# A block's last 16 keys: transposes and value matmuls over all 128 rows

## The chip, the cores and the metric

The kernel runs on one core of one Trainium2 chip. The metric is the time of one execution on the device in microseconds (us). The median of three runs of the kernel before is 1477.79 us (1477.2 to 1480.66). Engines are named as in the profile: PE (TensorE, matmuls), PEld (its weight loads), DVE (VectorE), ACT (ScalarE), POOL (GpSimd), SP (SyncE, which issues most DMAs).

## The reference

Two layers over 1040 tokens (16 learned ones and 1024 of the input) of width 1024. Each layer has a gated linear attention (GLA) and a sparse attention side by side; the part that matters here is the sparse attention:

```python
TOPK_MAX = 256; Q_BLOCK = 128; DSA_HEADS = 8; DSA_KV_HEADS = 2; DSA_HD = 64; N_META = 16
# for each block of 128 queries
score = einsum('bqj,bqjs->bqs', iw * 8 ** -0.5, relu(dots))          # indexer, all causal keys
_, sel = lax.top_k(score, topk)                                      # 256 keys of each query
s = einsum('bqgrd,bqkgd->bqgrk', qg, k_sel) * (DSA_HD ** -0.5)
p = softmax(where(valid, s, -inf))
o = einsum('bqgrk,bqkgd->bqgrd', p, v_sel)
# then: out projection, x <- LayerNorm(alpha * x + y)
```

The kernel does not gather: it computes all causal scores and gives the keys that were not selected a bias that makes their weight zero.

## The kernel before

The queries after the 16 learned tokens lie in 8 blocks `i` of 128. Block `i` sees 144 + 128 i keys: i + 1 whole blocks of 128 keys and a tail of 16, since keys are counted from token 0 and queries from token 16. The heads go in 4 pairs `hp`, so that a layer has 32 units `(i, hp)`, and the program 64. A unit has two stages:

- `stage_a` (line 1002): scores by matmuls (L1033, tile `S`), bias and row extreme on DVE (L1034), exponent on ACT (L1040). It leaves the weights of two heads in `Pt[0]`, `Pt[1]`: 128 rows (queries) by 144 + 128 i columns (keys).
- `stage_b` (line 1045), two units later: for every two key blocks, transposes of 128x128 pieces on PE (L1058, tile `PT`), a rounded copy `ph` on ACT (L1061), the remainder `pl` on DVE (L1062), and value matmuls of 128 contraction rows and 256 columns for each (L1064, L1065, tile `o`). Values `va[k]` stand with the rounded half in columns 0 to 63 and the remainder in 64 to 127.

The tail of 16 keys comes last in `stage_b` (lines 1066 to 1076). Only the last 32 queries of a block can see it, for the tail's first key is token 128 (i+1) and query row `r` is token 16 + 128 i + r. So the kernel takes rows 96 to 127 alone: two transposes of 32 rows and 16 columns (L1068, tile `PTe`, written 16x32), ACT copy and DVE remainder of 16x64 into one buffer `pe` (L1070, L1071), and two value matmuls of 16 contraction rows and 64 moving columns (L1074) that close the accumulation of `pos`. `pe` comes from the pool `v`, of which there are three buffers (`NV = 3`); the copies `ot` (L1077) and `rx` (L1086) come from it too.

Between the units PE has other work of the same layer to fill in: the gate projections `wz` (L356 to L358) and the first half of the output projection, `yg` and `yp` (L1128 to L1130). Products in single precision are made of three matmuls each, over a rounded part and a remainder.

The order of the instructions on each engine is not that of the code: a scheduler simulates the program while it is built and lets each engine's queue be filled in the order in which instructions become ready there. PE runs its queue in that order. Values are loaded by `vat` (lines 886 to 899): the last 16 keys' values are written to rows 0 to 15 of their piece alone (`m = 16`).

`rtok` (line 174) is a table of 144 columns in the tile of constants `cst` that the indexer's keys are rotated with, on DVE, at the start of each layer (L478 to L483). `r_g` is a large region that many stages use in turn: columns 3072 to 4095 hold the last of nine row tiles in the layer norms.

Of the kernel before, what the change touches and what calls it, by code (L numbers as in the profile page):

```python
# [10 lines left out]
F32 = mybir.dt.float32  # L11
F32R = mybir.dt.float32r
# [5 lines left out]
AF = mybir.ActivationFunctionType  # L18
OP = mybir.AluOpType
# [5 lines left out]
L = 1040  # L25
# [51 lines left out]
METAX = 21  # L77
METAL = 4
SWAP = 0
CST = 2450  # L80
NSEC = 5
FPRI = 4000
SELN = 256
# [15 lines left out]
def trunk(ctx: ExitStack, tc, a, out, dbg=None, stop=None):  # L99
    nc = tc.nc  # L100
    V, S, G, T, Q = nc.vector, nc.scalar, nc.gpsimd, nc.tensor, nc.sync
    dbg = dbg or {}

    const = ctx.enter_context(tc.tile_pool(name="const", bufs=1))
# [30 lines left out]
    def vu(name, dt=F32):  # L135
        return unit("v", dt)
# [6 lines left out]
    r_g = const.tile([128, 9328], F32, name="r_g")  # L143
# [14 lines left out]
    def small(n, dt=F32, parts=1):  # L158
        o = cofs[0]
        cofs[0] = o + n  # L160
        assert cofs[0] <= CST
        return cst[:, o:o + n].bitcast(dt) if dt != F32 else cst[:, o:o + n]

    ident = small(128)
# [6 lines left out]
    lmi = u("lmi", I32)[:, :448].rearrange("p (a b) -> p a b", a=7)  # L171
    Q.dma_start(lmi, a["lmask"])
    V.tensor_copy(lmask, lmi)
    rtok = small(144).rearrange("p (i j f) -> p i j f", i=2, j=9)
    Q.dma_start(rtok, a["rtok"])
    ropec, ropes = small(260), small(260)
    Q.dma_start(ropec, a["ropec"])
    Q.dma_start(ropes, a["ropes"])
# [33 lines left out]
    Q.dma_start(seltab, a["seltab"])  # L212
    selz, selc, selcap, selact = [seltab[:, 7 * x:7 * x + 7] for x in range(4)]
    iota8 = seltab[:, 28:36]
    nlev = [0]
    rr = [0, 0, 0, 0, 0, 0]
    sofs = [0]
    for i in range(NB):
        sofs.append(sofs[i] + (144 + 128 * i if i else 0))

    X = const.tile([128, 2, 8, L], F32R, name="X")
    h_dram = dpool.tile([L, D], F32, name="h_dram")
    z_dram = dpool.tile([8, 128, L], F32, name="z_dram")
    r_dram = dpool.tile([L, D], F32, name="r_dram")
# [187 lines left out]
    for l in range(DEPTH):  # L412
# [15 lines left out]
        for c0, n in GB:  # L428
            for f in range(2):
                p = sc("glog")  # L430
                T.matmul(p[:, :n], wg2[64:80, 128 * f:128 * f + 128], misc[64:80, c0:c0 + n], start=True, stop=True)
                e = log_sigmoid_parts(p[:, :n], bg[:, f:f + 1], 128, n)
                m = u("gmin")
# [14 lines left out]
        for j0, j1 in ((0, 5), (5, 9)):  # L448
            p = tr("mT")
# [6 lines left out]
            pv = p[:, 88 * (ja - j0):88 * (j1 - j0)].rearrange("p (j f) -> p j f", f=88)  # L456
            V.tensor_copy(ktm[:, ja:j1, :], pv[:, :, 0:64])
            V.tensor_scalar(iwt[:, ja:j1, :], pv[:, :, 80:88], 8 ** -0.5, 0.125, OP.mult, OP.mult)
        ikg = ikg_s
        for i, nm in enumerate(("idx_g", "idx_b")):  # L460
            v = a[nm][l]
            Q.dma_start(ikg[:, i, :], bass.AP(tensor=v.tensor, offset=v.offset, ap=[[0, 128], [1, 64]]))
# [25 lines left out]
        for js in ((0, 1, 2, 3, 4), (5, 6, 7, 8)):  # L488
            p = tr("ikT")
# [378 lines left out]
        with tc.high_priority(offset=SELPRI):  # L868
# [3 lines left out]
            for i in blks:  # L872
                W, x = 144 + 128 * i, slice(i - 1, i)
# [13 lines left out]
        va = []  # L887
        for k0, k1 in ((0, 4), (4, 5), (5, 8), (8, 9)):
            p = tr("vT")
            nk = k1 - k0  # L890
            m = 128 if k0 < 8 else 16
            o = 256 * (k0 % 5)
            vt = vat[k0 // 5][:, o:o + 256 * nk].rearrange("p (k g d) -> p k g d", g=2, d=128)
            va += [vt[:, k] for k in range(nk)]
            for k in range(k0, k1):
                T.transpose(p[:m, 128 * (k - k0):128 * (k - k0) + 128], avr[:, 128 * k:128 * k + m], ident)
            pv = p[:m, :128 * nk].rearrange("p (k g d) -> p k g d", k=nk, g=2)
            S.activation(vt[:m, :, :, 0:64], pv, AF.Copy)
            V.tensor_tensor(vt[:m, :, :, 64:128], pv, vt[:m, :, :, 0:64].bitcast(F32), OP.subtract)
# [145 lines left out]
        def stage_b(i, hp):  # L1045

            W, t0, g = 144 + 128 * i, NM + 128 * i, hp // 2
            b = ctxs[i]
            mx, oc, zt, Pt = b["mx"], b["oc"], b["zt"], b[hp]
            nk = i + 1  # L1050
            po = bank("o", NO, "o")
            pos = po[:, :256]
            for k0 in range(0, nk, 2):
                kk = min(2, nk - k0)
                p = pt_("PT")
                for x in range(kk):
                    for hh in range(2):
                        T.transpose(p[:, 256 * x + 128 * hh:256 * x + 128 * hh + 128],  # L1058
                                    Pt[hh][:, 128 * (k0 + x):128 * (k0 + x) + 128], ident)
                ph, pl = u("ph", F32R), u("pl", F32R)  # L1060
                S.activation(ph[:, :256 * kk], p[:, :256 * kk], AF.Copy)  # L1061
                V.tensor_tensor(pl[:, :256 * kk], p[:, :256 * kk], ph[:, :256 * kk].bitcast(F32), OP.subtract)  # L1062
                for x in range(kk):
                    T.matmul(pos, va[k0 + x][:, g, :], ph[:, 256 * x:256 * x + 256], start=(k0 + x == 0), stop=False)  # L1064
                    T.matmul(pos, va[k0 + x][:, g, :], pl[:, 256 * x:256 * x + 256], start=False, stop=False)  # L1065
            p = pt_("PTe")
            for hh in range(2):
                T.transpose(p[:16, 32 * hh:32 * hh + 32], Pt[hh][96:128, W - 16:W], ident[96:128, 96:128])  # L1068
            pe = vu("pe", F32R)
            S.activation(pe[:16, 0:64], p[:16, :64], AF.Copy)  # L1070
            V.tensor_tensor(pe[:16, 64:128], p[:16, :64], pe[:16, 0:64].bitcast(F32), OP.subtract)  # L1071
            pov = pos.rearrange("p (h t) -> p h t", h=2)
            for s in range(2):
                T.matmul(pov[:, :, 96:128], va[nk][:16, g, :],  # L1074
                         pe[:16, 64 * s:64 * s + 64].rearrange("p (h t) -> p h t", h=2),
                         start=False, stop=(s == 1))
            tt = vu("ot")  # L1077
            S.activation(tt[0:64, :256], po[64:128, :256], AF.Copy)
            for odd in range(2):
                V.tensor_tensor(oc[64 * odd:64 * odd + 64, hp, :], po[0:64, 128 * odd:128 * odd + 128],  # L1080
                                tt[0:64, 128 * odd:128 * odd + 128], OP.add)
            if hp < 3:
                return
            V.reciprocal(mx[:, :, 5:6], mx[:, :, 4:5])
            pr = pt_("rb")
            rx = vu("rx")  # L1086
            G.tensor_scalar(rx.rearrange("p (h d) -> p h d", h=8), mx[:, :, 5:6].to_broadcast([128, 8, 64]),
                            1.0, 0.0, OP.mult, OP.add)
            for j in range(4):
                T.transpose(pr[:, 128 * j:128 * j + 128], rx[:, 128 * j:128 * j + 128], ident)  # L1090
            prv = pr.rearrange("p (h t) -> p h t", h=4)
            if i < NDEF:
                V.tensor_tensor(oc, prv, oc, OP.mult)
                Q.dma_start(o_dram[i].rearrange("p (h t) -> p h t", h=4), oc)
                return
            V.tensor_tensor(zt, prv, zt, OP.mult)
            G.tensor_tensor(oc, oc, zt, OP.mult)
            S.activation(X[:, 0, 4:8, t0:t0 + 128], oc, AF.Copy)  # L1098
            G.tensor_tensor(X[:, 1, 4:8, t0:t0 + 128], oc, X[:, 0, 4:8, t0:t0 + 128].bitcast(F32), OP.subtract)
# [32 lines left out]
        for qd in range(NQ):  # L1132
            w = wunits(a["w_out"][l, qd], 256, 2, "wo", (0, 1))
            for j in tiles:
# [4 lines left out]
                p = bank("yg", NYG, "yg")[:n, :256]  # L1139
# [16 lines left out]
        for qd in range(2):  # L1156
            w = wunits(a["w_out"][l, qd], 256, 2, "wo", (2, 3))
            for j in tiles:
                t0, n = tok(j)
                p = pj("yp")[:n, :256]  # L1160
# [8 lines left out]
        for j in tiles:  # L1169
            t0, n = tok(j)  # L1170
            p = pj("yp")[:n]
# [99 lines left out]
```

## Time and profile before

| | us |
|---|---|
| median of three runs | 1477.79 |
| the profiled execution | 1479.79 |
| its span, first to last instruction | 1478.0 |
| PE busy | 1377.4 (93%) |
| weight loads busy | 1283.4 (87%) |
| DVE busy | 1040.1 (70%) |
| ACT busy | 791.7 (54%) |
| POOL busy | 721.3 (49%) |
| granted TensorE clock, mean | 0.974 |

The profiled execution is 2.0 us above the median; 1.8 us of it lie outside the span. The two attention stages, in which the units run, go from about 430 to 712 us and from about 1155 to 1421 us. A PE record's duration includes time in which the next matmul already runs, so the busy share of PE is no measure of how much it does; the distance from one start to the next is.

### The profile page before, as it was taken

To read this page: it belongs to the slowest core of one execution; us is meant where nothing else is said; L and a number is where in the kernel's file an instruction comes from. 1 tells how busy PE (TensorE), PEld (TensorE's weight loads), DVE (VectorE), ACT (ScalarE), POOL (GpSimd) and SP (SyncE) were. 2 spreads that over 40 slices of the span, in tenths; PEclk is the share of its full clock that TensorE was granted. 3 is DMA by queue.
4 is the path that set the end of the run, shared out by engine and by line. 5 is a ranking of instruction groups with operands and counts; after the bars stand their busy time and mean duration, and the time that the engine had idled before them with its cause. 6 is when DMAs were issued, how large, how long until landed. Compare 5 with 4: busy or idle time off the path is not lost. (4 is left out here: it accounts for less than half of the span.)

```text
span 1478.0 us, 27238 instructions
## 1 busy us (share of the span) xinstructions
PE 1377.4 (93%) x9471; PEld 1283.4 (87%) x9471; DVE 1040.1 (70%) x2440; ACT 791.7 (54%) x1815; POOL 721.3 (49%) x662
## 2 busy tenths in 40 slices
PE   2988998899999999999999889988999999999985
PEld 2878998788899988898999889987899999899985
DVE  8569997866534566776597699978665455778638
ACT  5446623544377777653254564254445877776412
POOL 6534422988643457222363441349785344652134
PEclk9999999999999999999999999999999999999998
DMA  7243322333243455215233432231433343621522
GB/s 256 105 133 87 93 96 77 98 95 117 83 126 116 120 149 141 67 48 165 70 128 109 133 99 74 94 104 51 146 101 105 103 135 108 186 90 51 158 69 114
DMA packets 143166, 162.63 MB, mean 110 GB/s; under 512 B 19552, under 2 KB 112496, under 8 KB 143024
## 3 DMA queue, kind: packets, MB, share of 16 engines
q1 hardware_dynamic: 112656, 125.73, 28.9%
q10 hardware_dynamic: 30368, 35.12, 6.9%
q8 instruction: 75, 1.23, 0.3%
q14 instruction: 67, 0.55, 0.1%
HBM read 104.76 MB, written 56.04 MB: 109 GB/s over the span
## 5 line engine op out<-in xcount | busy, mean ns | idle before, releaser
L323 POOL TENSOR_TENSOR w<-w 128x512 fp32r<-128x512 f32 (+1 forms) x134 | 181.3, 1354 | 294.2 <-ACT w L322 232.5
L322 ACT ACTIVATE w<-w 128x512 fp32r<-128x512 f32 (+1 forms) x134 | 83.5, 625 | 112.7 <-DMA w<-in_w_fm_dram 48.2
L543 DVE SCALAR_TENSOR_TENSOR r_sc<-v,cst,r_sc 128x346 f32<-128x346 f32 (+6 forms) x196 | 124.5, 689 | 5.8 <-ACT v L538 4.8
L356 PE MATMUL wz<-X,w 128*128 128x346 f32 (+1 forms) x384 | 125.9, 328 | 0.3
L357 PE MATMUL wz<-X,w 128*128 128x346 f32 (+1 forms) x384 | 125.0, 326 | 0.0
L358 PE MATMUL wz<-X,w 128*128 128x346 f32 (+1 forms) x384 | 124.6, 324 | 0.0
L1062 DVE TENSOR_TENSOR u<-PT,u 128x512 fp32r<-128x512 f32 (+1 forms) x160 | 100.7, 633 | 31.4 <-ACT u L1061 21.5
L1061 ACT ACTIVATE u<-PT 128x512 fp32r<-128x512 f32 (+1 forms) x160 | 86.0, 545 | 61.5 <-PE PT L1058 57.3
L635 POOL TENSOR_TENSOR qb<-r_g,u 64x256 f32<-64x256 f32 (+1 forms) x144 | 114.9, 798 | 5.6
L1040 ACT ACTIVATE r_g<-r_g,cst 128x272 f32<-128x272 f32 (+7 forms) x128 | 99.7, 780 | 10.7 <-DVE cst L1034 10.2
L538 ACT ACTIVATE v<-dots 128x346 f32<-128x346 f32 (+5 forms) x224 | 86.4, 461 | 16.3 <-PE dots L536 10.6
L1058 PE MATMUL PT<-cst,r_g 128*128 128x128 f32 x576 | 88.8, 277 | 0.0
L646 DVE COPY_PREDICATED r_g<-cst,lev 128x512 f32<-128x512 uint8 (+1 forms) x72 | 52.9, 735 | 50.1 <-PE lev L642 49.3
L570 PE MATMUL gvp<-w,X 128*128 128x256 f32 (+1 forms) x288 | 81.8, 289 | 1.5 <-ACT w L322 1.5
L629 POOL TENSOR_TENSOR r_g<-r_g,u 128x256 f32<-128x256 f32 (+1 forms) x60 | 49.6, 826 | 67.9 <-PE lev L642 40.5
L572 PE MATMUL gvp<-w,X 128*128 128x256 f32 (+1 forms) x288 | 82.6, 288 | 0.0
L571 PE MATMUL gvp<-w,X 128*128 128x256 f32 (+1 forms) x288 | 82.3, 287 | 0.0
L1033 PE MATMUL S<-ak,aq 128*128 128x346 f32 (+7 forms) x240 | 80.1, 340 | 0.2
L642 PE MATMUL lev<-qb,r_g 128*128 128x128 f32 (+1 forms) x480 | 66.8, 277 | 11.2 <-POOL qb L635 11.2
L642 PEld LDWEIGHTS lev<-qb,r_g 128*128 128x128 f32 (+1 forms) x480 | 60.0, 189 | 17.9 <-POOL qb L635 12.7
L1034 DVE CUSTOM_DVE_ANT_0 r_g<-S,r_kb 128x456 f32<-128x456 f32 (+6 forms) x112 | 55.9, 519 | 27.1 <-PE S L1033 20.2
L1128 PE MATMUL yp<-w,X 128*128 128x256 f32 (+1 forms) x238 | 69.1, 292 | 5.6 <-ACT X L1098 5.6
(351 smaller groups left out, 4966.0 us busy)
## 6 DMA issues: line engine op xcount, KB each, us to landing
w<-in_w_fm_dram SPq DMA_DIRECT2D x88, 256.0 KB
r_g<-aq_dram SPq DMA_DIRECT2D x64, 128.0 KB
w<-in_w_out_dram SPq DMA_DIRECT2D x32, 256.0 KB
r_sc<-h_dram SPq DMA_DIRECT2D x53, 128.0 KB
h_dram<-r_g SPq DMA_DIRECT2D x12, 512.0 KB
r_dram<-r_sc SPq DMA_DIRECT2D x48, 128.0 KB
r_sc<-z_dram SPq DMA_DIRECT2D x22, 256.0 KB
z_dram<-zu ACTq DMA_DIRECT2D x32, 173.0 KB
```

The costliest lines, as they stand in the source:

```text
L323: G.tensor_tensor(lo[:, :n], raw[:, :n], hi[:, :n].bitcast(F32), OP.subtract)
L356: T.matmul(p[:m, :n], wh, xh, start=(k == 0), stop=False)
L357: T.matmul(p[:m, :n], wh, xl, start=False, stop=False)
L358: mm = T.matmul(p[:m, :n], wl, xh, start=False, stop=(k == 7))
L538: S.activation(rl[:, :n], p[:, :n], AF.Relu)
L543: V.scalar_tensor_tensor(sco[:, c:c + n], rl[:, :n], w, sco[:, c:c + n], OP.mult, OP.add)
L635: eng.tensor_tensor(qb[P, :, o].rearrange("p c (b m) -> p c b m", m=m), qv[P, :, 1, :].rearrange("p (c b) m -> p c b m", c=nch), Ev[P, :, ...
L642: T.matmul(pv[:, ch], kst, qb[:, ch], start=True, stop=True)
L1040: ins = S.activation(P[:, :W], P[:, :W], AF.Exp, bias=mx[:, h, nci - 1:nci], scale=-1.0, accum_out=mx[:, h, 4:5]).ins
L1058: T.transpose(p[:, 256 * x + 128 * hh:256 * x + 128 * hh + 128], Pt[hh][:, 128 * (k0 + x):128 * (k0 + x) + 128], ident)
L1061: S.activation(ph[:, :256 * kk], p[:, :256 * kk], AF.Copy)
L1062: V.tensor_tensor(pl[:, :256 * kk], p[:, :256 * kk], ph[:, :256 * kk].bitcast(F32), OP.subtract)
```

## The change

The transposes of the tail take all 128 rows and write 16x128 each. ACT and DVE read the last 32 columns of each out of them, as before. The rounded part and the remainder go to rows 0 to 15 of a buffer of 128 rows; there are two such buffers (`pez`), filled with zeros once at the start and used in turn (`rr[2]`), in place of buffers of the pool `v`. The value matmuls contract over 128 rows: rows 16 to 127 of the value piece are set to zero once per layer, and those of `pez` stay zero. The results are the same numbers.

The buffers lie behind `X` in one tile, 256 columns more. To make room, `rtok` leaves the constants and is loaded in each layer, ahead of the indexer norm's two vectors, into `r_g[:, 3584:3728]`; the tile of constants becomes 272 columns smaller.

```diff
-CST = 2450
+CST = 2178
...
-    rtok = small(144).rearrange("p (i j f) -> p i j f", i=2, j=9)
-    Q.dma_start(rtok, a["rtok"])
+    rtok = r_g[:, 3584:3728].rearrange("p (i j f) -> p i j f", i=2, j=9)
...
+    xt = const.tile([128, 16 * L + 256], F32R, name="X")
+    X = xt[:, :16 * L].rearrange("p (s k t) -> p s k t", s=2, k=8)
+    pez = [xt[:, o:o + 128].rearrange("p (s t) -> p s t", s=2) for o in (16 * L, 16 * L + 128)]
+    for x in range(2):
+        V.tensor_scalar(xt[:, 16 * L + 128 * x:16 * L + 128 * x + 128], ident, 0.0, None, OP.mult)
...
+        Q.dma_start(rtok, a["rtok"])
         for i, nm in enumerate(("idx_g", "idx_b")):
...
+            if m < 128:
+                for g in range(2):
+                    V.tensor_scalar(vt[:, 0, g], ident, 0.0, None, OP.mult)
...
             for hh in range(2):
-                T.transpose(p[:16, 32 * hh:32 * hh + 32], Pt[hh][96:128, W - 16:W], ident[96:128, 96:128])
-            pe = vu("pe", F32R)
-            S.activation(pe[:16, 0:64], p[:16, :64], AF.Copy)
-            V.tensor_tensor(pe[:16, 64:128], p[:16, :64], pe[:16, 0:64].bitcast(F32), OP.subtract)
+                T.transpose(p[:16, 128 * hh:128 * hh + 128], Pt[hh][:, W - 16:W], ident)
+            rr[2] = 1 - rr[2]
+            pe = pez[rr[2]]
+            pv = p[:16, :256].rearrange("p (h t) -> p h t", h=2)[:, :, 96:128]
+            hi, lo = [pe[:16, x].rearrange("p (h t) -> p h t", h=2) for x in range(2)]
+            S.activation(hi, pv, AF.Copy)
+            V.tensor_tensor(lo, pv, hi.bitcast(F32), OP.subtract)
             pov = pos.rearrange("p (h t) -> p h t", h=2)
             for s in range(2):
-                T.matmul(pov[:, :, 96:128], va[nk][:16, g, :],
-                         pe[:16, 64 * s:64 * s + 64].rearrange("p (h t) -> p h t", h=2),
+                T.matmul(pov[:, :, 96:128], va[nk][:, g, :], pe[:, s].rearrange("p (h t) -> p h t", h=2),
                          start=False, stop=(s == 1))
```

The scheduler works anew on the changed program. PE has the same number of matmuls, in an order that differs in many places. Line numbers in the changed kernel are higher by 8 to 10 in `stage_b` and after it.

Here PE's queue stands near the end of the second layer's attention, before the change: a tail's transposes (`PTe`), the next block's transposes and value matmuls, and a tail's two value matmuls (the row `o<-v,vb` of 128x2x32).

```order
L1065 MATMUL o<-u,va 128x256
L1068 MATMUL PTe<-cst,r_g 16x32 x2
L1064 MATMUL o<-u,va 128x256
L1033 MATMUL S<-ak,aq 128x346
L1033 MATMUL S<-ak 128x346
L1065 MATMUL o<-u,va 128x256
...
L1064 MATMUL o<-u,vb 128x256
L1065 MATMUL o<-u,vb 128x256
L1074 MATMUL o<-v,vb 128x2x32 x2
L1058 MATMUL PT<-cst,r_g 128x128 x8
```

The same place after the change:

```order
L1073 MATMUL o<-u,va 128x256
L1076 MATMUL PTe<-cst,r_g 16x128 x2
L1072 MATMUL o<-u,va 128x256
L1041 MATMUL S<-ak,aq 128x346
L1041 MATMUL S<-ak 128x346
L1073 MATMUL o<-u,va 128x256
...
L1072 MATMUL o<-u,vb 128x256
L1073 MATMUL o<-u,vb 128x256
L1085 MATMUL o<-X,vb 128x2x32 x2
L1066 MATMUL PT<-cst,r_g 128x128 x4
```

The tail's matmuls stand where they stood; four of the eight transposes behind them have moved ahead of them.

Here SP's queue stands at the start of the second layer, before the change (`h_dram<-r_g` are the stores of the first layer's result rows, `w` are weights):

```order
L1182 DMA h_dram<-r_g 128x1024
L600 DMA r_g<-bc_dram 128x16
L1182 DMA h_dram<-r_g 128x1024
L321 DMA w<-in_w_fm_dram 128x512 x3
L375 DMA r_g<-iq_dram 64x1x260 x2
```

And after it:

```order
L1192 DMA h_dram<-r_g 128x1024
L605 DMA r_g<-bc_dram 128x16
L1192 DMA h_dram<-r_g 128x1024
L464 DMA r_g<-in_rtok_dram 128x144
L325 DMA w<-in_w_fm_dram 128x512 x2
```

The load of `rtok` stands between the store of the last row tile, whose columns it overwrites, and three loads of weights, of which one has moved further back.

Here DVE's queue stands at the very start of the changed program: the two blocks of zeros for `pez` (L219) have come between the conversion of a mask (L173) and the first layer norm's statistics, which followed each other before.

```order
L191 MEMSET cst 128x1
L173 CAST cst<-u 128x448
L219 TENSOR_SCALAR X<-cst 128x128 x2
L276 BN_STATS cst<-r_sc 16x6 x2
L277 BN_AGGR cst<-cst 16x2
```

They read `ident`, whose load has moved ahead of the input rows in SP's queue.

## Rows read from the trace of the kernel before

**Rows 1.** Busy time by stage: PE, PEld, DVE, ACT, POOL in turn, then clock, DMA.
```profile
430.00:712.00 282.00, 277.54 (x1954) 255.47 (x1953) 175.53 (x538) 186.59 (x434) 116.87 (x107) 0.99 0.40 119
1155.00:1421.00 266.00, 259.52 (x1821) 240.87 (x1821) 167.66 (x502) 175.35 (x400) 111.16 (x101) 0.98 0.41 117
```

**Rows 2.** The tail's matmuls by line: count, ns min/median/max, first and last start, forms.
```profile
L1068 PE MATMUL PTe<-cst,r_g x128: 188/192/193, 432.0 to 1405.6; 32*16 32x32 f32 x128
...
L1074 PE MATMUL o<-v,va x64: 271/292/293, 439.2 to 1279.9; 16*128 16x64 f32 x64
L1074 PE MATMUL o<-v,vb x64: 271/292/293, 575.0 to 1407.8; 16*128 16x64 f32 x64
```

**Rows 3.** PE's timeline (start, length in us): tail transposes standing alone, first and last.
```profile
442.00 0.22 PE L1068 MATMUL PTe<-cst,r_g 32*16 32x32 f32 x2
...
1405.34 0.28 PE L1065 MATMUL o<-u,va 128*128 128x256 f32 x1
1405.55 0.22 PE L1068 MATMUL PTe<-cst,r_g 32*16 32x32 f32 x2
...
1405.93 0.28 PE L1130 MATMUL yp<-w,X 128*128 128x256 f32 x1
1406.05 0.28 PE L1128 MATMUL yp<-w,X 128*128 128x256 f32 x1
```

**Rows 4.** PE's timeline: a tail's two value matmuls together, the first of their kind.
```profile
439.03 0.28 PE L1065 MATMUL o<-u,va 128*128 128x256 f32 x1
439.24 0.41 PE L1074 MATMUL o<-v,va 16*128 16x64 f32 x2
...
439.84 0.32 PE L356 MATMUL wz<-X,w 128*128 128x346 f32 x1
```

**Rows 5.** PE's timeline: one of a tail's value matmuls alone, the first.
```profile
452.59 0.32 PE L358 MATMUL wz<-X,w 128*128 128x346 f32 x1
452.75 0.32 PE L356 MATMUL wz<-X,w 128*128 128x346 f32 x1
452.99 0.29 PE L1074 MATMUL o<-v,va 16*128 16x64 f32 x1
...
453.47 0.32 PE L358 MATMUL wz<-X,w 128*128 128x346 f32 x1
```

**Rows 6.** PE's timeline: value matmuls with the next tail's transposes between, the first.
```profile
448.63 0.28 PE L1065 MATMUL o<-u,va 128*128 128x256 f32 x1
448.84 0.29 PE L1074 MATMUL o<-v,va 16*128 16x64 f32 x1
448.85 0.22 PE L1068 MATMUL PTe<-cst,r_g 32*16 32x32 f32 x2
...
449.44 0.32 PE L356 MATMUL wz<-X,w 128*128 128x346 f32 x1
```

**Rows 7.** PE's timeline: a transpose of 128 rows and 16 columns.
```profile
598.59 0.27 PE L956 MATMUL PmT<-cst,v 128*16 128x128 f32 x1
598.70 1.03 PE L1058 MATMUL PT<-cst,r_g 128*128 128x128 f32 x8
```

**Rows 8.** PE's timeline: two matmuls over 128 contraction rows with 16 moving columns.
```profile
580.51 0.28 PE L1130 MATMUL yg<-w,X 128*128 128x256 f32 x1
580.63 0.28 PE L945 MATMUL Sm<-ak,mq 128*128 128x16 f32 x2
...
581.07 0.29 PE L1074 MATMUL o<-v,vb 16*128 16x64 f32 x1
```

**Rows 9.** Who waited for the tail's ACT copy L1070 (us, times).
```profile
  PEld o L1074: 0.3, 1
```

**Rows 10.** SP's and DVE's timeline: the last row's store, the next load, the table's reader.
```profile
779.28 0.38 SPq L1182 DMA_DIRECT2D h_dram<-r_g  x1
...
813.27 0.22 DVE L478 TENSOR_TENSOR r_g<-r_g,cst 128x72 f32<-128x72 f32 x1
```

**Rows 11.** DVE's timeline at the start: the first statistics of the layer norm.
```profile
4.81 1.27 DVE L272 BATCH_NORM_STATS2 cst<-r_sc 16x6 f32<-16x512 f32 x2
```

More of the change, by code (lines that the diff above doesn't have):

```diff
@@ L219, in trunk @@
         sofs.append(sofs[i] + (144 + 128 * i if i else 0))
-    X = const.tile([128, 2, 8, L], F32R, name="X")
     h_dram = dpool.tile([L, D], F32, name="h_dram")
```

## The prediction

> **What bounds the kernel now.** I read the table of stages first, since the change lies in the two attention stages alone. There PE is busy 277.5 of 282 us and 259.5 of 266 us, at a granted clock of 0.99 and 0.98, while DVE and ACT are near two thirds and POOL near two fifths [rows 1]. So PE sets the pace of both stages: it always has a gate projection or a piece of the output projection to go on with. What PE's queue holds there counts in full, and work on the other engines counts only where PE comes to wait for it.
>
> The busy share does not tell how much of PE's time is work, so next come the tail's own instructions, by line. 128 transposes of 32 rows and 128 value matmuls of 16 rows, from 432.0 to 1407.8 us [rows 2]: four per unit, 64 units. Their listed durations (0.19 and 0.29 us) overlap with their neighbours' and say nothing on the cost. That is read from the distance of starts in PE's timeline, and the reader should see this there: between full-height matmuls of 256 columns the starts lie 0.12 us apart (1405.93 to 1406.05, [rows 3]), at 346 columns 0.16 (452.59 to 452.75, [rows 5]). Where a tail comes, the step into it and the step out of it are both longer. I call what a tail adds, beyond the full-height matmuls around it, its price: the time from the start of the last matmul before it to the start of the second one after it, less the plain steps of the matmul before it and the one behind it.
>
> - Two transposes alone: 1405.34 to 1405.93 is 0.59, less 0.12 and 0.12 gives 0.35 us, though the two themselves take only 0.22 from first start to last end [rows 3]. There are 47 such pairs (442.00 is the first), together 16.4.
> - Two value matmuls together: 439.03 to 439.84 is 0.81, less 0.12 and 0.16 gives 0.53 [rows 4]; 27 such pairs, together 14.3.
> - One value matmul alone: 452.75 to 453.47 is 0.72, less 0.16 and 0.16 gives 0.40 [rows 5]. There are 45; between transposes they are cheaper by 0.03, so I take 0.38 as their mean: 17.1.
> - Value matmul, the next tail's two transposes, value matmul: 448.63 to 449.44 is 0.81, less 0.12 and 0.16 gives 0.53 for all four [rows 6]; 13 of them, 6.9.
> - The rest, by the same reading of the timeline: five single transposes (0.34 each) and six instructions in two mixed groups (0.5 a group), 2.7.
>
> The sum is 57.4 us of PE's time for 256 small matmuls, 0.22 each. Full-height ones of 256 columns take 0.12.
>
> **The change part by part.** *Transposes.* Each now has 128 rows, 16 stationary columns and 128 moving ones. The trace has this very form once between full-height neighbours: the transpose at 598.59 is followed by the next start after 0.11 [rows 7], with no longer step behind it. 128 of them: 14.1 us.
>
> *Value matmuls.* Each now has 128 contraction rows and still 64 moving columns. That form is not in the trace, but it lies between two that are. With 16 columns and full height, two of them (580.63) stand between 580.51 and 581.07: 0.56, less 0.12 for the matmul before them and 0.21 for the step into a tail that follows (439.03 to 439.24, [rows 4]) leaves 0.23, so 0.12 each [rows 8]. With 256 columns it is 0.12 too [rows 3]. I take 0.117, and 128 of them cost 15.0. From below, 0.03 is the least that a small matmul has taken (two transposes in 0.22, of which one lasts 0.19, [rows 2, 3]); from above, 0.22, the mean price of the old form, were there nothing to the height. By these ends the 128 cost 4 to 28, and the time lies between 1440 and 1464; the value taken is the one that rows on either side of the form give.
>
> Together 29.1 in place of 57.4: PE has 28.3 us less to do, half in each stage. The argument rests on the steps into and out of a tail: they come with a change of height, not of kind, for a full-height transpose of 16 columns goes straight on to the next matmul.
>
> The Trainium skill, in "TensorE: Matmul & The Clock Gate", section "Why this matters for your kernels", says that a small matmul of few contraction rows takes as long as one of 128, and that the gain of few rows is that they run beside others in other rows. By this rule the change would save nothing and lose the overlap. The trace has that overlap in the mixed groups, where a transpose starts 0.01 us after a value matmul [rows 6]; it does not have the equal time, since the steps around a tail are longer. What the rule would make of the sum is the first rival below.
>
> *Evacuation.* ACT and DVE still handle 16x64 elements per unit, read with a stride. I cost this at nothing: PE has waited for this copy once, 0.3 us in all [rows 9], and in the new order the tail's value matmuls still stand a similar number of matmuls behind its transposes. Bounds: a slower strided read of 0.1 us would be hidden by the same matmuls; uncovered in every unit, it would be 6.4. Leaving the pool `v` can only free its buffers earlier.
>
> *The table `rtok`.* One more small load in each layer, queued on SP behind the store issued at 779.28; its reader on DVE runs at 813.27 [rows 10]. The weight loads behind it wait for that store. 34 us cover store and load, so nothing; if the three weight loads behind it came late, PE would stand for as long, which I bound by 2 us.
>
> *Zeros.* Four writes of 128x128 on DVE in the layers are hidden behind PE. The two at the start are not: they stand ahead of the first statistics, which start at 4.81 [rows 11], and wait for a load that is now the third in the queue. The start is a chain of layer norms without PE work beside it. I take 0.5 us lost, between a gain of 1 (the identity arrives earlier for the first transposes) and a loss of 2 (1.3 us for one more tile's statistics ahead, [rows 11], and the zeros).
>
> *Order.* The queue's order changes in many places. At those shown the tail stands as before and some transposes trade places, which changes no count of full-height work. With 5% less PE work in these stages, DVE and ACT come nearer to PE. PE stood idle 4.5 and 6.5 us in them [rows 1]; I allow 1 us more, bounded by doubling that idle time (11 us more).
>
> Sum: the profiled execution of 1479.8, less 28.3, plus 0.5 and 1, gives 1453.0. That execution was 2.0 above the median of the three runs, so the forecast for the median is 1451.
>
> **The rivals.** *The steps belong to the shortness of the matmuls, not to their height* (slower). Then all long steps stay, the value matmuls cost what they did, and a transpose, with 128 moving columns instead of 32, takes 0.11 instead of 0.03: 128 times 0.08 is 10 us more. In the 13 mixed groups the two transposes were free beside the value matmuls (0.53 with or without them, [rows 4, 6]); at full height they are not, which adds about 0.35 for each, 4.6. Time: 1477.8 plus 14.6 plus 1.5, 1494. For it: value matmuls follow a fresh DVE result, and the step out of them is 0.2 whatever comes. Against: [rows 7, 8], short and full-height matmuls without such steps. Between this case and the forecast lie 42.9 us of steps (28.3 and 14.6); the change is slower if less than a third of them goes.
>
> *Only the transposes lose their steps.* Then 47 pairs fall from 0.35 to 0.22 and five single ones from 0.34 to 0.11, some 7.3, while the 13 mixed groups lose 0.22 each by the lost overlap, 2.9. That leaves 4.4 of gain, less 1.5 for start and waits: 1475. For it: no row has a full-height matmul with 64 columns. Against: it would have to cost more than both the 16 and the 256 columns around it.
>
> *The work goes, but PE comes to wait in the units.* If in the new order each tail's value matmuls or the next block's come 0.2 us too early for ACT and DVE, 64 units lose 12.8: 1464. For it: ACT and DVE carry the same work in less time. Against: two thirds busy at most, and 0.3 us of such waits before [rows 1, 9].
>
> **How the numbers follow.** The forecast has a chance of 0.76, PE's new waits 0.12, transposes alone 0.06, the slower case 0.04; 0.02 is left for a new order that loses elsewhere what the tails gain. The likeliest is 1451. Its own range is 1445 to 1458: the value matmuls' lower end is not near, so I go down by the gain at the start, a luckier order and part of the 0.117, and up by the bounds of start and idle time. To hold the time 8 times in 10 it reaches up into the case of waits: 1443 to 1465. Differences below 0.3%, 4.4 us, can't be told from none by such runs. Faster than that are the forecast, the waits and a third of the transposes-alone case: 0.90. The same: the rest of that case and half of the remainder, 0.05. Slower: 0.05.
>
> **What would show it.** In PE's timeline after, the step from a full-height matmul into a tail's transposes is 0.12, not 0.21, and the next start after them comes without a longer second step; a pair's price is 0.22 and that of two value matmuls 0.23. The lines of the tail list 128 rows. Each attention stage is 13 to 14 us shorter, and the stages outside them keep their length within 2 us. PE's idle time in the attention stages is under 7 us each. The forecast is wrong if steps of 0.2 us remain around the tails, or if PE's waits for the tail's copies or for `u` grow to several us in a stage.

## The result and the profile after

The changed kernel took 1461.5 us (median of four runs, 1460.1 to 1464.0) against 1477.5 for the kernel before, a ratio of 0.9886, 95% interval 0.9872 to 0.9899. So it is faster by 16 us. The forecast was 1451, a gain of 26.5: the sign was right, and 10 us of the gain did not come. The time lies in the range that was to hold it 8 times in 10, 1443 to 1465, but above the forecast's own range, 1445 to 1458. The profiled execution took 1461.0, and its span is 1459.2. Two executions of some 2.6 ms, one of this kernel when it ran again and one of another kernel below, count in none of the ratios.

The stages, over the same two stretches and with the same columns as in [rows 1] (busy PE, PEld, DVE, ACT, POOL, then clock and DMA):

```profile
430.00:712.00 282.00, 270.38 (x2008) 260.53 (x2008) 180.77 (x546) 185.98 (x434) 118.88 (x108) 0.98 0.40 118
1155.00:1421.00 266.00, 255.60 (x1916) 248.81 (x1914) 168.51 (x502) 169.40 (x381) 110.92 (x101) 0.98 0.39 118
```

More matmuls fit into each stretch (2008 for 1954, 1916 for 1821), and yet PE stands idle longer: 11.6 us where it was 4.5, and 10.4 where it was 6.5. Both things happened at once, and they have to be read apart.

First the work. The tail's matmuls by line, which answer to [rows 2]:

```profile
L1076 PE MATMUL PTe<-cst,r_g x128: 270/272/421, 431.3 to 1386.8; 128*16 128x128 f32 x128
...
L1085 PE MATMUL o<-X,va x64: 192/196/278, 437.6 to 1263.2; 128*128 128x64 f32 x64
L1085 PE MATMUL o<-X,vb x64: 191/196/400, 565.5 to 1389.8; 128*128 128x64 f32 x64
```

PE's timeline at a pair of transposes alone (start and length in us), to be held against [rows 3]:

```profile
1386.53 0.28 PE L1073 MATMUL o<-u,va 128*128 128x256 f32 x1
1386.65 0.38 PE L1076 MATMUL PTe<-cst,r_g 128*16 128x128 f32 x2
1386.79 0.37 PE L1139 MATMUL yp<-w,X 128*128 128x256 f32 x1
1386.99 0.28 PE L1140 MATMUL yp<-w,X 128*128 128x256 f32 x1
```

The step into the tail is 0.12, as between full-height neighbours, and 1386.53 to 1386.99 is 0.46; less 0.12 and 0.12, the pair's price is 0.22, where it was 0.35. Two value matmuls together, against [rows 4]:

```profile
437.44 0.28 PE L1073 MATMUL o<-u,va 128*128 128x256 f32 x1
437.56 0.31 PE L1085 MATMUL o<-X,va 128*128 128x64 f32 x2
437.70 0.40 PE L360 MATMUL wz<-X,w 128*128 128x346 f32 x1
437.94 0.32 PE L361 MATMUL wz<-X,w 128*128 128x346 f32 x1
```

0.50, less 0.12 and 0.16, is 0.22, where it was 0.53. One value matmul alone has a median price of 0.09 over 63 of them; the 45 of before had 0.37 [rows 5]. Summed by these medians over all groups, the 256 small matmuls cost 25.5 us; by the same count they cost 56.9 before. So PE has 31 us less to do, a little more than the 28.3 forecast.

Then the waits. PE's waits by the line that waits, what it waited for, us in total, times, longest:

```profile
PE o L1072 <- DVE u L1070: 7.4, 2, 4.1
...
PE o L1072 <- ACT u L1069: 3.6, 6, 0.9
PE o L1073 <- DVE u L1070: 2.1, 6, 0.6
```

Before, the block's value matmuls had waited 2.2 us in all for ACT's `u`, the longest time 1.3. Now they wait 13 for ACT's and DVE's, and over half of that is in two waits, one in each stage. The accounts of the two attention stages follow, from the first tail transpose to the last value matmul, worked out from the starts of all their matmuls (us, both stages added up). A plain step is the usual distance from one start to the next at that number of columns; the tail's small matmuls are counted in that line with about 0.1 each.

| | before | after |
|---|---|---|
| length | 525.9 | 509.2 |
| the plain steps of all matmuls | 483.7 | 484.0 |
| what steps of up to 0.25 us over the plain one add | 37.4 | 6.5 |
| longer gaps, in which PE waits | 4.8 | 18.7 |

31 us of work gone, 14 us of waits come: 17 us gained in the stages. The rest of the 18.8 us between the two spans lies outside them.

Two terms are needed for the long wait of the first stage. `h` stands for the layer's input rows, to which the output projection is added tile by tile: SP loads a tile of them (L1148), DVE adds to it (L1151), SP stores it in `r_dram` (L1152). The first three query blocks are deferred: their attention is kept in DRAM, and a function `cat` later loads it with its gate `z`, and POOL multiplies the two. Followed back in the timelines of SP's queue, POOL, ACT, DVE and PE (start, length, and in brackets the idle time before and what ended it):

```profile
565.72 0.55 SPq L1152 DMA_DIRECT2D r_dram<-r_sc  x1
...
568.42 0.32 SPq L1148 DMA_DIRECT2D r_sc<-h_dram  x1
568.86 0.92 SPq L927 DMA_DIRECT2D r_sc<-z_dram  x2
...
571.90 1.26 POOL L931 TENSOR_TENSOR r_sc<-r_sc 128x512 f32<-128x512 f32 x1 [6.82 <-DMA r_sc<-z_dram]
...
573.19 0.63 ACT L933 ACTIVATE X<-r_sc 128x512 fp32r<-128x512 f32 x1 [4.90 <-POOL r_sc L931]
...
574.66 0.57 ACT L1069 ACTIVATE u<-PT 128x512 fp32r<-128x512 f32 x1
...
575.26 0.69 DVE L1070 TENSOR_TENSOR u<-PT,u 128x512 fp32r<-128x512 f32 x1 [5.35 <-ACT u L1069]
...
576.01 0.39 PE L1072 MATMUL o<-u,va 128*128 128x256 f32 x1 [4.08 <-DVE u L1070]
```

This is to be read from the top. SP's queue stands at the load of `h` (L1148) until the store of 565.72 has landed. The load of `z` for a deferred block's gating (`cat`, L927) is queued behind it. POOL multiplies when `z` is there, ACT copies the product into `X` (L933), and only behind that and an exponent of 0.93 us in ACT's queue comes the copy of `PT` (L1069) without which PE has no next matmul. The chain itself is not new. This is the same place before:

```profile
578.06 1.29 POOL L923 TENSOR_TENSOR r_sc<-r_sc 128x512 f32<-128x512 f32 x1 [3.99 <-DMA r_sc<-z_dram]
...
579.38 0.63 ACT L925 ACTIVATE X<-r_sc 128x512 fp32r<-128x512 f32 x1 [1.45 <-POOL r_sc L923]
...
581.46 0.69 DVE L1062 TENSOR_TENSOR u<-PT,u 128x512 fp32r<-128x512 f32 x1 [1.84 <-ACT u L1061]
...
582.29 0.36 PE L1064 MATMUL o<-u,va 128*128 128x256 f32 x1
```

DVE had finished `u` at 582.15, and PE used it at 582.29 without a wait: 4.2 us from POOL to PE there, 4.1 here. But PE now gets to this place 10 us earlier, and the chain, which hangs on SP's queue, only 6.2. The 4 us between them are the wait. Not all of the 10 us is lost work: 12 matmuls of `yg`, 1.4 us, that stood ahead of this place stand behind it in the new order.

The wait costs more than its own length, as the stretches around it show (columns as in [rows 1]):

```profile
565.00:571.50 6.50, 6.50 (x55) 6.32 (x54) 4.31 (x15) 2.33 (x7) 0.07 (x1) 1.00 0.64 166
571.50:576.00 4.50, 0.43 (x5) 0.19 (x3) 0.74 (x2) 2.81 (x6) 3.84 (x4) 1.00 0.35 101
576.00:580.00 4.00, 3.78 (x18) 3.54 (x19) 3.54 (x12) 3.47 (x9) 3.92 (x4) 0.57 0.48 142
580.00:584.00 4.00, 4.00 (x35) 3.85 (x34) 1.96 (x5) 2.81 (x6) 2.43 (x3) 1.00 0.26 74
```

Behind the idle time the granted clock is 0.57 for 4 us, mostly the lower level of 1.2 GHz, and 18 matmuls pass where 35 do in the next 4 us. At 0.57 of the clock, 4 us do the work of 2.3: by this estimate some 1.7 us more are lost.

### The profile page after: what moved, and what is told of

Same layout as the page of the kernel before. It is cut to its first block, busy times and chain, and to the rows that moved or that the text cites. A ratio compares the mean times of both kernels' runs of the same rounds, so it can differ in the third digit from the quotient of the medians.

```text
span 1459.2 us, 27163 instructions
## 1 busy us (share of the span) xinstructions
PE 1349.8 (93%) x9471; PEld 1278.6 (88%) x9471; DVE 1028.7 (71%) x2446; ACT 791.3 (54%) x1815; POOL 722.2 (49%) x662
## 5 line engine op out<-in xcount | busy, mean ns | idle before, releaser
L1070 DVE TENSOR_TENSOR u<-PT,u 128x512 fp32r<-128x512 f32 (+1 forms) x160 | 100.6, 634 | 44.7 <-ACT u L1069 33.5
L640 POOL TENSOR_TENSOR qb<-r_g,u 64x256 f32<-64x256 f32 (+1 forms) x144 | 110.5, 767 | 6.3 <-PE lev L647 0.6
L1069 ACT ACTIVATE u<-PT 128x512 fp32r<-128x512 f32 (+1 forms) x160 | 85.7, 545 | 40.9 <-PE PT L1066 31.7
L577 PE MATMUL gvp<-w,X 128*128 128x256 f32 (+1 forms) x288 | 81.7, 286 | 0.0
L576 PE MATMUL gvp<-w,X 128*128 128x256 f32 (+1 forms) x288 | 81.3, 284 | 0.0
L575 PE MATMUL gvp<-w,X 128*128 128x256 f32 (+1 forms) x288 | 80.6, 286 | 0.0
L1072 PE MATMUL o<-u,va 128*128 128x256 f32 x240 | 70.1, 304 | 10.1 <-DVE u L1070 7.4
L647 PEld LDWEIGHTS lev<-qb,r_g 128*128 128x128 f32 (+1 forms) x480 | 61.7, 194 | 15.7 <-POOL qb L640 10.4
```

What stands on the lines that cost most here:

```text
L640: eng.tensor_tensor(qb[P, :, o].rearrange("p c (b m) -> p c b m", m=m), qv[P, :, 1, :].rearrange("p (c b) m -> p c b m", c=nch), Ev[P, :, ...
L647: T.matmul(pv[:, ch], kst, qb[:, ch], start=True, stop=True)
```

## The experiments

The first four ran on one chip (the kernel before took 1481.2 there). "Steps" and "waits" are the last two lines of the table above, for the profiled execution of each kernel.

| | ratio, 95% interval | steps | waits |
|---|---|---|---|
| transposes only | 0.9995, 0.998 to 1.001 | 35.9 | 12.4 |
| value matmuls only | 0.9859, 0.9838 to 0.9879 | 15.8 | 10.8 |
| neither | 0.9990, 0.9976 to 1.0003 | 35.6 | 6.4 |
| the change, gating later | 0.9830, 0.9811 to 0.9850 | 7.6 | 15.7 |

**Transposes only.** The buffers stay; the value matmuls go back to 16 rows.

```diff
-                T.matmul(pov[:, :, 96:128], va[nk][:, g, :], pe[:, s]...
+                T.matmul(pov[:, :, 96:128], va[nk][:16, g, :], pe[:16, s]...
```

> The changed kernel with the value matmuls of the tail back at 16 contraction rows (the new buffers and the moved table stay). Theory (the steps belong to a change of height): pairs of transposes fall from a price of 0.35 to 0.22, the mixed groups lose their overlap; 4 us of PE's time less than before, 1472 to 1475 us, and the steps of 0.2 us around the value matmuls remain. Rival (a new order or the freed pool buffers made most of the gain): near 1462, like the changed kernel.

No gain: 1481.6 us, where 1472 to 1475 were expected. The first pair of value matmuls shows that their old steps are back, 0.21 into them and 0.34 to the next start:

```profile
436.41 0.28 PE L1073 MATMUL o<-u,va 128*128 128x256 f32 x1
436.62 0.41 PE L1085 MATMUL o<-X,va 16*128 16x64 f32 x2
436.96 0.43 PE L360 MATMUL wz<-X,w 128*128 128x346 f32 x1
```

Summed by medians the small matmuls cost 55.3, only 1.6 less than before: a pair of transposes alone fell from 0.35 to 0.22, but where a value matmul stands ahead of one, the three cost 0.54, and the 13 groups in which transposes had been free beside value matmuls are gone. The waits rose by more than that. So transposes at full height bring nothing while the value matmuls stay short.

This kernel also tells how much of the waits is order. PE's queue in it is that of the whole change, matmul for matmul, and so are those of SP, DVE and POOL. Its work is only 1.6 us less than before, and yet PE waits for `u` at the same two places, 3.9 and 2.0 us, where it did not before:

```profile
PE o L1072 <- DVE u L1070: 5.9, 2, 3.9
```

In all it waits 12.4 us, against 4.8 before and 18.7 in the change. By these single executions more than half of the new waits come with the new order, and not because PE has less to do.

**Value matmuls only.** The transposes go back to 32 rows.

```diff
-                T.transpose(p[:16, 128 * hh:128 * hh + 128], Pt[hh][:, W - 16:W], ident)
+                T.transpose(p[:16, 128 * hh + 96:128 * hh + 128], Pt[hh][96:128, W - 16:W], ident[96:128, 96:128])
```

> The changed kernel with the transposes of the tail back at 32 rows. Theory: the value matmuls alone carry most of the gain; the traced changed kernel has two of them at about 0.11 in place of 0.53, so some 19 us of PE's time go, and 5 to 7 are given back in waits: 1463 to 1469 us. Rival (both parts are needed, since any change of height left in a unit brings the drain back): 1472 or more.

1462.8 us, as much gain as the whole change: the rival, that both parts are needed, falls. The small matmuls cost 34.9 by medians, 22.0 less than before and 9.4 more than in the whole change; the waits are 8 us less than there. PE's steps around the short transposes are the old ones (0.33 from the first start of a `PT` pair to the transposes, 0.15 behind them):

```profile
440.90 0.40 PE L1066 MATMUL PT<-cst,r_g 128*128 128x128 f32 x2
441.23 0.22 PE L1076 MATMUL PTe<-cst,r_g 32*16 32x32 f32 x2
441.38 0.40 PE L1041 MATMUL S<-ak,aq 128*128 128x272 f32 x1
441.62 0.29 PE L1041 MATMUL S<-ak 128*128 128x272 f32 x1
```

The 9.4 us of work that the full-height transposes save did not reach the time: in the whole change PE waits 8 us longer, in the other order that comes with these transposes.

**Neither.** Both lines go back; buffers, zeros, the place of `rtok` and the order that follows from them stay.

> All that the change does but for the heights: buffers of their own for the tail, zeros, the table loaded in each layer, and a new order, with transposes of 32 rows and value matmuls of 16. Theory: none of this is worth anything, within 4 us of the kernel before (1474 to 1482). Rival (order and buffers make the gain): 1470 or less.

1479.2 us, no difference. Everything that the change does beside the height of the matmuls costs and brings nothing that can be measured. The order that comes with full-height transposes is not among it.

PE's order is here that of the value matmuls only, but for 26 of 9471 places. So the waits can be set side by side (us, one execution each):

| | value matmuls of 16 rows | of 128 |
|---|---|---|
| transposes of 32 rows, and their order | 6.4 | 10.8 |
| transposes of 128 rows, and their order | 12.4 | 18.7 |

By these, the value matmuls' 22 to 30 us of work bring 4 to 6 us of waits, and the step to full-height transposes with their order brings 6 to 8, though without the value matmuls it saves PE only some 2 us of work.

**Gating later.** The whole change, and in the table that says after which unit a deferred block is gated, block (1, 1) and its two followers move three units on.

```diff
-CATX = {... 20: ((0, 8), (1, 1),), 21: ((1, 2), (1, 3),)}
+CATX = {... 20: ((0, 8),), 23: ((1, 1),), 24: ((1, 2),), 25: ((1, 3),)}
```

> The changed kernel with the first three query blocks' results put into X later: after units 23, 24 and 25 instead of 20, 21 and 21. Theory: the two longest new waits of PE (4.1 and 3.3 us) come from ACT, whose queue stands at the copy of such a result while POOL waits for the load of its gate; moved away from there, both go, and the kernel takes 1453 to 1457 us, PE's idle time in each attention stage at 5 us or less. Rival (the lost time is the general lateness of ACT and DVE once PE is faster): the wait turns up elsewhere, 1459 to 1464.

1456.4 us, 8 us better against its own runs of before than the change against its own (0.983 and 0.9886); against the change's second measurement below, 0.9863, it is 5 us, and the intervals overlap. The two waits of 4.1 and 3.3 us are gone, but others came: 3.7 us at 1288.7, for POOL, which stood behind a late weight load. The theory had the right place; that the waits as a whole would go was too much.

The second four ran together (before: 1480.7).

| | ratio, 95% interval | steps | waits |
|---|---|---|---|
| the change, `h` later | 0.9805, 0.978 to 0.983 | 7.5 | 14.3 |
| the change, `h` and gating later | 0.9792, 0.9767 to 0.9816 | 6.4 | 12.3 |
| before, gating later | 0.9987, 0.9974 to 1.0001 | 34.6 | 5.7 |
| value matmuls only, gating later | 0.9872, 0.9847 to 0.9898 | 12.2 | 13.5 |

**`h` later.** The whole change; five buffers for `h` stay, but a load is issued behind the store of four tiles earlier, not at once behind the store whose buffer it takes, which lands some 2.7 us later.

```diff
+        rst = []
...
-                Q.dma_start(hp, h_dram[t0:t0 + n, 256 * qd:256 * qd + 256])
+                hl = Q.dma_start(hp, h_dram[t0:t0 + n, 256 * qd:256 * qd + 256]).ins
+                if len(rst) > 3:
+                    hold(hl, rst[-4])
...
+                rst.append(Q.dma_start(r_dram[...], hp).ins.name)
```

> The changed kernel; only the loads of h for the output projection are issued behind the store of four tiles earlier instead of at once behind the store whose buffer they take (five buffers), so that SP's queue no longer stands about 2.7 us for that store to land with the loads of z behind it. Theory (the tails' work is gone, and what is missing of the gain was lost where PE caught up with the loads of z for the deferred blocks, stuck in SP's queue): SP's waits ahead of the h loads between 540 and 580 us fall from 13.4 to under 4 us, the z load that PE waited for at 576 goes out about 2 us earlier, PE's long waits of 4.1 and 3.3 us shrink to about 2 or less, and the ratio to the kernel before is 0.984 to 0.987. Rival (ACT and POOL themselves set the pace of these blocks, the queue only stands because it has time): the h loads go earlier, PE's waits stay at 10 to 11 us a stage, and the ratio stays at 0.9886, that of the change.

1452.6 us, better than the theory had it. What SP's queue waited for, first in the change from 540 to 580 us (us, times, longest):

```profile
SPq L1148 <- DMA r_dram<-r_sc: 13.4, 7, 2.9
```

and in this kernel from 530 to 580:

```profile
SPq L1149 <- DMA r_dram<-r_sc: 0.4, 1, 0.4
```

The loads of `z` that PE had to wait for go out 5.2 us earlier (563.70 for 568.86), and POOL's multiplication runs 2.6 us earlier, at 569.35; what holds POOL for the rest the profile puts down to another load into the same tile:

```profile
563.70 1.86 SPq L927 DMA_DIRECT2D r_sc<-z_dram  x2
...
569.35 1.29 POOL L931 TENSOR_TENSOR r_sc<-r_sc 128x512 f32<-128x512 f32 x1 [3.54 <-DMA r_sc<-h_dram]
```

PE's waits for `u`, by line:

```profile
PE o L1072 <- ACT u L1069: 5.0, 6, 1.4
...
PE o L1073 <- DVE u L1070: 2.0, 6, 0.7
...
PE o L1072 <- DVE u L1070: 0.8, 1, 0.8
```

7.4 us in two waits became 0.8 in one. PE's queue is in the order of the change, so for these two waits the rival, that ACT and POOL set the pace themselves, falls. The profiled execution took 1457.7 us, the second longest of six, so it shows only part of the 9 us by which the medians differ.

**Both later.** The two edits together, on the changed kernel.

> The changed kernel with both: the deferred blocks' gating three units later (as in the earlier run that moved it) and the h loads behind an older store. Theory: both take away the same kind of wait, so together PE's waits in the two stages, 15.7 us with the moved gating alone, fall to 10 or less, and the ratio is 0.979 to 0.982. Rival (the waits have other causes and turn up elsewhere when the queue is freed): 0.983 as with the moved gating alone.

1451.3 us, the fastest of all kernels here, with the fewest waits of the versions in which all tails are at full height; 12.3 us of them were not the 10 or less expected, and its interval overlaps that of `h` later alone.

**Before, gating later.**

> The kernel before, with the deferred blocks' gating three units later and nothing else. Theory (the waits exist only since PE got faster): PE waited only 4.8 us in both stages of the kernel before, 1.5 of them at this place, so the move is worth 0 to 2 us here: ratio 0.998 to 1.000. Rival (the move is worth its 5 to 8 us in any kernel, and tells nothing of the change): 0.9945 to 0.997.

1479.3 us: nothing that can be measured, as the theory said. The same move brought the changed kernel 5 to 8 us.

**Value matmuls only, gating later.**

> Full-height value matmuls with the old 32-row transposes, and the deferred blocks' gating three units later. Without the move this kernel stood at 0.9859, as good as the whole change. Theory (full-height transposes save PE 7 to 8 us of steps, which waits ate): with the waits moved out of the way the short transposes show again, and this kernel is 3 to 7 us slower than the whole change with the same move (0.983): 0.985 to 0.988. Rival (the transposes' height is worth nothing in any case): 0.983, equal to it.

0.9872, inside what the theory expected, yet not for its reason. The waits did not go: they are 13.5, more than without the move (10.8), and the time is no shorter than without it (0.9859). So the move does not pay wherever PE is early, and this run does not show how the short transposes come out with the waits away, and only the price by medians, 9.4 us of PE's work, speaks for full height there.

The last three ran together (before: 1479.9).

| | ratio, 95% interval | steps | waits |
|---|---|---|---|
| before, `h` later | 0.9968, 0.9955 to 0.9980 | 36.0 | 3.4 |
| before, `h` and gating later | 0.9994, 0.9980 to 1.0008 | 35.4 | 7.1 |
| the change again | 0.9863, 0.9842 to 0.9884 | 7.5 | 20.8 |

> The kernel before, with nothing but the h loads behind the store of four tiles earlier (the edit that brought the changed kernel to 0.9805). Theory (the stand of SP's queue cost the old kernel nothing, since PE had the tails' steps to cover it): SP's waits for the store fall from about 15 us to under 2 here too, PE's waits stay near 4 us in both stages, and the ratio is 0.997 to 1.000. Rival (the stand cost every kernel the same 8 to 12 us, and the change only happens to be measured without it): 0.992 to 0.995.

4.7 us faster, slightly more than expected and about half of what the same edit gave the changed kernel. SP's wait for the store, 15.5 us over 40 us of the kernel before, went here as well, and from 540 to 590 us the queue stands for DVE instead, so the old kernel had cover for part of it:

```profile
SPq L1145 <- DVE r_sc L1144: 10.4, 7, 2.2
...
SPq L1139 <- DMA r_dram<-r_sc: 0.4, 1, 0.4
```

> The kernel before with both edits: the deferred blocks' gating three units later and the h loads behind an older store. Against the changed kernel with both (0.9792) this gives what the change is worth when SP's queue is free in both. Theory: 0.996 to 1.000 here, so the change is worth 25 to 30 us there, as PE's work says (28). Rival (part of the gain of the two edits has nothing to do with the change): 0.988 to 0.993, which would leave the change 13 to 20 us, as measured without them.

> The changed kernel itself, on the chip and beside the runs of the two kernels above. Both theories: 0.987 to 0.990, as the first time; a ratio nearer 0.981 would mean that the two edits' gain over the change was a difference of chips.

Nothing for both edits on the kernel before, so the 4.7 us of `h` later alone do not show there. The change ran again at 0.9863, a shade under the 0.987 to 0.990 expected, with an interval that overlaps the first. With these the change can be priced four times, each kernel with the change against the same kernel without it (difference of the two ratios, times 1480):

| | without | with the change | worth, us |
|---|---|---|---|
| as they are | 1 | 0.9886, 0.9863 | 17 to 20 |
| gating later | 0.9987 | 0.9830 | 23 |
| `h` later | 0.9968 | 0.9805 | 24 |
| both | 0.9994 | 0.9792 | 30 |

Each is uncertain by 3 to 4 us, and the two rows between can't be told from each other. With both edits the change brings about what was forecast as its work, 28 us; as it stands, about a third of that is lost.

## Why the prediction was right, and where it was not

- *The bound.* Right: PE set the pace of the attention stages before, and less work there made them shorter. Not seen was how near the next bound lay: not DVE, ACT or POOL by their busy shares, but a chain through SP's queue, POOL and ACT that is hidden as long as PE comes late to it, by its work or by its order.
- *Transposes at 0.11.* Right to a hundredth: a pair costs 0.22. One sign did not come: the second step behind them is still longer, 0.20 for 0.12 (1386.79 to 1386.99). It only makes up for a step of 0.03 just ahead of it, and the same 0.20 follows the eight full-height transposes of [rows 7] (599.49 to 599.70).
- *Value matmuls at 0.117.* Right as a pair (0.22 for 0.23 forecast); alone they are cheaper, 0.09. Together the work fell by 31 us where 28.3 were forecast. The rows on either side of the unseen form gave the price.
- *The steps come with a change of height.* Shown from both sides: with 16 rows the value matmuls keep their long steps, with 128 and the same 64 columns they lose them. For the transposes the moving columns changed with the rows, so they show less. The first rival, shortness, falls. What was said for it, that the step out of a value matmul is 0.2 whatever comes, misreads [rows 6], where a short transpose starts 0.01 behind one. What the Trainium skill says in "TensorE: Matmul & The Clock Gate", section "Why this matters for your kernels", that few contraction rows take as long as 128, does not hold for these small matmuls among full-height ones: 0.37 at 16 rows, 0.09 at 128.
- *Only the transposes lose their steps.* The second rival, 1475, was the wrong way round: by themselves the transposes brought nothing, and the value matmuls by themselves as much as the whole change.
- *Evacuation, `rtok`, zeros, and the start.* Costed at nothing and 0.5: the version with all of them and neither edit of height is at 0.9990. Right within what can be measured.
- *Order, and PE's new waits: 1 us.* This is the step that failed. It was sized by the waits of before and by busy shares of two thirds; the term measured 14 us (18.7 for 4.8), more than the bound of 11 put on it, and part of the steps at half clock comes on top. By the prediction's own signs it failed too: PE stands idle 11.6 and 10.4 us where under 7 were said, and waits for `u` 7.1 and 6.1 us in the two stages. The third rival, that the work goes and PE comes to wait, gave 1464 at a chance of 0.12 and is near what happened; but its mechanism, 0.2 us in each of 64 units, was not: over half of the new waits are two of 3 to 4 us, each behind a load of `z`, with some shorter ones around them and at the end of each stage. Nor do they come from the lost work alone. The new order was taken to change little; run with the old value matmuls, it has 12.4 us of waits already. The trace of before told how near they were: at this place DVE had finished 0.14 us before PE used its result, and ACT had stood 1.45 us for POOL. There was no cover to lose, however idle the engines were on average.
- *Each attention stage 13 to 14 us shorter.* 7.5 and 9.2: wrong by the same waits. The stages outside kept their length within 2 us.
- *The range.* 1461.5 is in the range of 1443 to 1465 only because that reached up to the third rival. It is no support for the sum, which had the waits 13 us too small and the work saved 3 us too small.

What stays open: how the waits divide between order and lost work beyond single executions (the change has 18.7 us in one and 20.8 in the other); why `h` later alone brings 9 us by the medians while its profiled execution shows 3 to 6 of them, and whether the gaps at the last unit of each stage, 2 us each, could be filled.

## What to carry to other kernels

When the engine that sets the pace is to lose some of its work in a stretch, its own idle time says nothing about the cover that goes: list the chains that end shortly before it needs them (here load, POOL, ACT, DVE, PE), take the slack of each, and compare it with what the engine will have gained by then. A new order counts as well, for it can bring the engine to such a place earlier with the same work; a version in the new order that keeps the old cost tells the two apart. A load that waits on an in-order queue for a store just issued holds up everything queued behind it; give it a store or two of distance, even with the same number of buffers. And a small matmul among tall ones is priced by the starts around it: at full height, with zeros for the rest, it can cost less than half of the short one.

## What the runs showed of the hardware

- Two full-height matmuls of 64 columns between full-height neighbours cost PE 0.22 us together and one alone 0.09; at 16 rows they cost 0.53 and 0.37.
- The step from a full-height matmul of 256 columns into a tail is 0.21 us where the tail has 16 or 32 rows and 0.12 where it has 128. The second step behind a pair is 0.10 longer than plain with few rows and still 0.08 longer with 128.
- Transposes at 128 rows next to value matmuls at 16 took 1.6 us off the 56.9 of PE's work; value matmuls at 128 rows next to transposes of 32 took 22.0 off it.
- After PE stood idle from about 571.9 to 576.0, the granted clock was 0.57 over the next 4 us and 1.00 again from 580; before the idle time it was 1.00.
- A store of 128x256 from SP's queue held up the load that takes its buffer for up to 2.9 us, seven times in 40 us and 13.4 us in all; with one more store between them it was 0.4 us in 50.
